# Order of two products of a pair in the feed forward, small compression products issued two at a time, and a shorter planning distance in the memory attention

## The chip, the cores and the metric

One Trainium2 chip, one core. The time is device microseconds (us) of one execution, the median over the runs shown. The work is spread by hand over TensorE (matrix products, PE in the profile; PEld is its weight load), VectorE (DVE), ScalarE (ACT), GpSimd (POOL) and SyncE (SP), which issues the transfers from memory.

## The reference, cut to what matters

Two models run one after the other on a 512 x 1024 activation: two layers of a first model, then a block of a second. The change touches three pieces of the second one.

```python
def _compress(tok, pos_emb, w1, w2):            # 512 tokens -> 31 blocks of 32 tokens
    idx = np.arange(n_cmp)[:, None] * CMP_STRIDE + np.arange(CMP_LEN)[None, :]
    blocks = tok[:, idx] + pos_emb
    hid = jax.nn.gelu(blocks.reshape(B, n_cmp, CMP_LEN * hd) @ w1)
    return hid @ w2

def _memory_attention(h, mem, g_q, g_kv, w_q, w_kv, w_o):   # 4 heads, 256 memory rows
    q = (_rmsnorm(h, g_q) @ w_q).reshape(B, S, MEM_HEADS, MEM_HEAD_DIM)
    kv = (_rmsnorm(mem, g_kv) @ w_kv).reshape(B, M, 2, MEM_HEADS, MEM_HEAD_DIM)
    pr = jax.nn.softmax(jnp.einsum('bshd,bmhd->bhsm', q, kv[:, :, 0]) * MEM_HEAD_DIM ** -0.5)
    o = jnp.einsum('bhsm,bmhd->bshd', pr, kv[:, :, 1])
    return o.reshape(B, S, MEM_HEADS * MEM_HEAD_DIM) @ w_o

def _swiglu(u, w_in, w_out):                    # D_FF = 2816, 22 blocks of 128
    a = u @ w_in
    return (jax.nn.silu(a[..., :D_FF]) * a[..., D_FF:]) @ w_out
```

## The kernel before, in words

Activations lie transposed, as eight tiles of 128 features x 512 tokens. A weight unit is a `raw` tile of 128 x 1024 that SyncE loads; ScalarE rounds it into `whi`, VectorE or GpSimd takes the rest into `wlo`, and each product of full precision is three products of TensorE: `xh,whi`, `xl,whi` and `xh,wlo`, accumulated in a bank of PSUM. Banks have three tags: three `mm`, four `x`, one `o`. Five stages follow each other: A and C (the first model), B (the mixer of the second), Q (memory attention), F (feed forward).

The whole program is planned while it is built. `Build` holds a model of the engines with a cost for every operation. The order on TensorE comes from the code: between two steps of a long projection `mms` calls `tick`, and there a generator waiting in `active` or `queue` (a step of some attention, say) may put its own products in. It may when `at(a) + self.margin <= self.now`: its inputs and a free bank must be there, by the model, at least `margin` ahead. `margin` is 2000 ns everywhere (`MARGIN`). Where no projection is left to hide behind, `drain` forces the steps. The other engines' orders come from a second pass (`again`), which works back from the end, gives every operation a latest time, and lets each engine take the most urgent one that is ready; additions and subtractions may land on VectorE or GpSimd. So any change of TensorE's order can move operations of the other engines far around it.

Three places matter.

`compress` (stage B, in `phase_b`), run for keys and for values: 16 products of 31 columns in single precision, `w1` (tiles `cw`) against the blocks `bl` (tile `blk`), into one bank with the tag x. In the trace each such product is two passes.

`phase_q` (stage Q): the two query projections `mq`, then `chain(j, i0)` four times (heads pair j, half i0 of the tokens): logits `ps_x<-memk,mq`, maximum, exponential, sum and scaling of `e` on VectorE and ScalarE, transposes `ps_x<-ident,e`, copies `pt`, products with the values `ps_o` or `ps_mm<-pt,memv`. Two projections of the memory (`mkv` 2 and 3, products `mxh,whi` of 256 columns) and the transposes of their result (`mvt`) come in the same stage.

`pair` (stage F): 17 pairs of units of the feed forward (`fa`, `fb`) are computed with seven products of 256 columns in place of eight. Each product n is 12 instructions of TensorE (4 x 3). `x[n]` holds its moving side (made once by `side`: `th`, `tl`, and for product 4 `zh`, `zl`), `it[n]` its weights (`wsh`, `wsl` for 6, 7 and 3, `whi`, `wlo` for the rest). Products 2 and 3 share a bank ("c"), 5 and 4 share another ("d"). After each product its result is added on VectorE: after 5, q's second half is `p + u` (in the trace `pp<-ps_x,pp`); after 3, t1 = bank c + q; after 4, t2 = bank d + u. Besides, two output products of the feed forward (`ps_mm<-acth,woh` and so on) stand between pairs.

Of the kernel before, what the change touches and what calls it, by code (L numbers as in the profile page):

```python
# [44 lines left out]
NEVER = 1e15  # L45
IDLE = {"V": 0.0, "A": 0.0, "G": 0.0, "D": 2150.0}
LOOK, NORMED_A = 2, 14
MARGIN = 2000.0
MEM_FROM, MEM_B = ("up", 1, 0), 2

QUEUED = {"V": 300, "A": 200}
# [278 lines left out]
class Build:  # L330
# [3 lines left out]
    def __init__(self, ctx, tc, aps, out):  # L334
# [7 lines left out]
        self.conc = 4  # L342
        self.margin = MARGIN
        self.o_free = PSUM_BUFS["o"]
# [564 lines left out]
    def pair(self, it, x, nxt):  # L909

        V, A = self.V, self.A
        a, b = slice(0, 256), slice(256, 512)
        if nxt:
            self.sums(nxt)
            self.whole(nxt, 0)
        while len(x[4]) < 4:
            assert self.force(), it["keys"]
        bank = lambda: self.p(min(("mm", "x"), key=lambda t: min(map(self.free, self.slots[t]))))
        t1, t2, q = self.t("pr"), self.t("pr"), self.t("pp")
        u = self.t("pp")  # L920
        banks = {}
        for n, name, c in ((1, "1", a), (2, "c", a), (6, "6", a), (5, "d", b), (7, "7", a), (4, "d", a), (3, "c", b)):
            if name not in banks:
                banks[name] = bank()
            p = banks[name]
            hi, lo = it.pop(n)
            for k in range(4):
                xh, xl = x[n][k]
                self.T.matmul(p[:, c], hi[:, k], xh, start=k == 0, stop=False)
                self.T.matmul(p[:, c], hi[:, k], xl, start=False, stop=False)  # L930
                self.T.matmul(p[:, c], lo[:, k], xh, start=False, stop=k == 3)
                self.tick()
            self.rank += EVAC
            if n == 1:
                A.copy(q[:, a], p[:, a])
            elif n == 6:
                V.tensor_add(u[:, a], p[:, a], q[:, a])
            elif n == 5:
                V.tensor_add(q[:, b], p[:, b], u[:, a])
            elif n == 7:  # L940
                V.tensor_add(u[:, b], p[:, a], u[:, a])
            elif n == 4:
                two = lambda t: t.rearrange("p (h c) -> p h c", h=2)
                V.tensor_add(two(t2), two(p), u[:, None, b].to_broadcast([P, 2, 256]))
            elif n == 3:
                V.tensor_add(t1, p, q)
            self.rank -= EVAC
            if n == 2:
                if nxt:
                    self.whole(nxt, 1)  # L950
                else:
                    self.ahead()
        return t1, t2
# [740 lines left out]
    def phase_b(self, h, prev):  # L1694
# [291 lines left out]
        def compress():  # L1986
            yield "need", ("r", "kvc")
            kvc = T["kvc"]
            w2, hidden, kv = self.t("cw2"), self.t("hid"), self.t("kvc")
            w2k, w2v = w2[:, :P], w2[:, P:P + 64]  # L1990
            self.dma(w2k, self.aps["cw2k"])
            self.dma(w2v, self.aps["cw2v"])
            hid, hu = (hidden[:, 64 * n:64 * n + 64].rearrange("p (b n) -> p b n", b=2) for n in range(2))
            hv4 = hidden[:, P:2 * P].rearrange("p (h n) -> p h n", h=4)
            kc.append(kv[:, :32])
            vc.append(kv[:, 32:288].rearrange("p (h n) -> p h n", h=4))
            G.memset(hid, 0.0)
            G.memset(vc[0], 0.0)
            for b in range(2):
                st, bl = self.t("cst"), self.t("blk")  # L2000
                r = slice(64 * b, 64 * b + 64)
                self.dma(st[:64], kvc[r])
                self.dma(st[64:, :S - 1], kvc[r, 1:])
                yield "on", st
                src = bass.AP(tensor=st.tensor, offset=st.offset, ap=[st.ap[0], [2, 16], [16, 31]])
                V.tensor_add(bl[:, :496].rearrange("p (l n) -> p l n", l=16), src,
                             col["pos_k" if b == 0 else "pos_v"][:, :, None].to_broadcast([P, 16, 31]))
                w1 = [self.t("cw1") for _ in range(4)]
                for c in range(4):
                    self.dma(w1[c].rearrange("p (l m) -> p l m", l=4),  # L2010
                                        self.aps["cw1k" if b == 0 else "cw1v"][:, 4 * c:4 * c + 4])
                yield "on", w1, bl
                p = self.p("x")
                for l in range(16):
                    mm(p[:, :31], w1[l // 4][:, (l % 4) * P:(l % 4 + 1) * P], bl[:, l * 31:(l + 1) * 31],
                       start=l == 0, stop=l == 15)
                V.tensor_copy(hid[:, b, :31], p[:, :31])
                yield
            V.tensor_mul(hu, hid, hid)
            V.tensor_scalar(hu, hu, 0.044715, 1.0, op0=OP.mult, op1=OP.add)  # L2020
            V.tensor_mul(hu, hu, hid)
            A.activation(hu, hu, AF.Tanh, scale=math.sqrt(2.0 / math.pi))
            V.scalar_tensor_tensor(hu, hu, 1.0, hid, op0=OP.add, op1=OP.mult)
            V.tensor_scalar_mul(hid, hu, 0.5)
            V.tensor_copy(hv4, hid[:, 1:2, :].to_broadcast([P, 4, 32]))
            yield "on", hid, hv4
            p = self.p("x")
            mm(p[:, :32], w2k, hid[:, 0], start=True, stop=True)
            V.tensor_copy(kc[0], p[:, :32])
            p = self.p("x")  # L2030
            mm(p[:, :64], hidden[:, P:2 * P], w2v, start=True, stop=True)
            for hh in range(4):
                V.tensor_copy(vc[0][32 * hh:32 * hh + 32, hh], p[32 * hh:32 * hh + 32, :64])
            yield "done", "kc"
            yield
# [105 lines left out]
        for w in MAIN_B.split():  # L2141
            k = int(w[-1]) if w[-1].isdigit() else 0
            n = w.rstrip("0123")
# [27 lines left out]
        for w in BACK_B.split():  # L2171
            k = int(w[-1]) if w[-1].isdigit() else 0
            n = w.rstrip("0123")
            if n == "st":
                for i in range(4):
                    self.add(stick(k, i), ("ka", k))
                self.add(tok(("va", k), ("van", k)), ("va", k))
            elif n == "tw":
                self.add(tok("vwgt", "vwg"), "vwgt")
            elif n == "tb":  # L2180
                self.add(tok("vbs", "vbn"), "vbs")
            elif n == "se":
                self.add(select(k), "vwg")
            elif n == "dsa":
                for i in range(4):
                    self.add(dsa(k, i), ("qb", k))
            elif n == "cp":
                self.add(compress(), "kvc")
                for i in range(4):
                    self.add(cmp_gen(i), "kvc")  # L2190
            elif n == "nsa":
                for i in range(4):
                    n = 4 * k + i - LOOK
                    self.add(nsa(k, i), "ksw" if n < 0 else ("npv", n // 4, n % 4))
# [15 lines left out]
    def phase_q(self, h, prev):  # L2210
        mm = self.T.matmul
        V, A = self.V, self.A
        x, rb = self.start(h, prev, self.col["norm_mq"], EPS6, "norm_q")
        self.conc = 4
        D, y = {}, {}
        halves = (slice(0, 64), slice(64, 128))

# [61 lines left out]
                self.add(chain(j, i0), ("mq", j))  # L2279
        self.tasks([(("mq", j), None, functools.partial(q_task, j)) for j in range(2)] + self.mem_tasks(range(MEM_B, 4)))  # L2280
        self.drain()
        hi, lo = self.unit(("mo", 0))
        begun = [self.p("mm") for _ in range(PSUM_BUFS["mm"] - 1)]
        for j, p in enumerate(begun):
# [17 lines left out]
    def phase_f(self, h, prev):  # L2302
# [58 lines left out]
        self.start_now(norm_x())  # L2361
        self.tasks([((key, f), None, functools.partial(into, f, key)) for f in range(PLAIN) for key in ("fa", "fb")][:-1])
        pairs = [pair(f) for f in range(PLAIN, FF)]
        self.sums(pairs[0])
        for _ in into(PLAIN - 1, "fb"):
# [117 lines left out]
```

## Time and profile before

| | |
|---|---|
| median of 3 runs | 1486.21 us (1485.58 to 1487.2) |
| the profiled execution | 1487.19 us, its span 1485.3 us |
| TensorE busy | 1460.9 us, 98% of the span, 8452 products |
| VectorE, ScalarE, GpSimd busy | 1075.7, 780.6, 366.4 us |
| granted TensorE clock, mean | 0.994 of full speed |
| chain that ended last | TensorE 87%, VectorE 7%, ScalarE 3% |

A row of a stage says how long the stretch is and how much of it each engine was busy; the length less PE's number is the time in which TensorE stood still. PEclk is the granted clock: 1.00 is 2.4 GHz, 0.50 is 1.2 GHz. In a timeline, brackets hold the idle time just before an instruction and the engine that ended it. Almost all instructions carry one line of a helper, so tiles tell them apart.

### The profile page before, as it was taken

The numbers are of one execution on the slowest core, as the hardware profiler recorded it, in microseconds if no ns is written. First come the engines' busy times: TensorE is split into PE (matmuls) and PEld (weight loads), VectorE is DVE, ScalarE is ACT, GpSimd is POOL, SyncE is SP. The second block draws the span as 40 slices with busy tenths as digits, with TensorE's granted clock in tenths as the row PEclk, the third lists the DMA queues.
The fourth block names the chain that finished last, engine by engine and source line by source line (L and its number), as shares of the span: only waits on it lengthen the run. The fifth ranks groups of instructions, "written<-read, shape, count | busy, mean of one in ns | idle before, by whom it ended". The sixth has DMA issues, their size and how long they took to land.

```text
span 1485.3 us, 22690 instructions
## 1 busy us (share of the span) xinstructions
PE 1460.9 (98%) x8452; PEld 1247.2 (84%) x8452; DVE 1075.7 (72%) x2081; ACT 780.6 (53%) x1548; POOL 366.4 (25%) x267
## 2 busy tenths in 40 slices
PE   8999999999999999999999999999999999999997
PEld 6888888888888888888887888888878899999986
DVE  6997877556535587666989994756566888877755
ACT  5553557555523588744688335754355544444324
POOL 1272612010100010000343030302015668532310
PEclk9999999999999999999999999999999999999998
DMA  6222222322332311124424331223312232332221
GB/s 218 85 72 71 80 92 71 100 85 86 114 114 100 103 64 65 58 96 139 123 89 129 119 118 61 86 72 132 124 57 88 83 128 93 107 128 100 75 82 58
DMA packets 53358, 143.52 MB, mean 97 GB/s; under 512 B 6848, under 2 KB 11968, under 8 KB 53248
## 3 DMA queue, kind: packets, MB, share of 16 engines
q1 hardware_dynamic: 53248, 142.07, 28.8%
q8 instruction: 67, 1.10, 0.3%
q14 instruction: 43, 0.35, 0.1%
HBM read 128.81 MB, written 4.19 MB: 90 GB/s over the span
## 4 chain that ended last, share of the span: by engine, by line
PE 87%; DVE 7%; ACT 3%; issue 1%; DMA 1%; POOL 0%; SPq 0%; POOLq 0%; DVEq 0%; ACTq 0%
PE ps_mm L595 64%; PE ps_x L595 19%; PE ps_o L595 4%; DVE sc L595 1%; ACT su L595 1%; DVE wlo L595 1%; DMA rpu<-rpr 1%; ACT e L595 1%; DVE sr L595 0%; ACT se L595 0%; ACT sr L595 0%; DVE e L595 0%; ACT whi L595 0%; DVE cv L595 0%; DVE m L595 0%
## 5 line engine op out<-in xcount | busy, mean ns | idle before, releaser
L595 PE MATMUL ps_mm<-xh,whi 128*128 128x512 f32 x936 | 383.7, 410 | 0.1
L595 PE MATMUL ps_mm<-xh,wlo 128*128 128x512 f32 x936 | 367.3, 392 | 0.0
L595 PE MATMUL ps_mm<-xl,whi 128*128 128x512 f32 x936 | 366.6, 392 | 0.0
L595 ACT CAST whi<-raw 128x1024 fp32r<-128x1024 f32 x199 | 208.7, 1052 | 256.3 <-issue 130.6
L595 DVE TENSOR_TENSOR wlo<-raw,whi 128x1024 fp32r<-128x1024 f32 x162 | 209.1, 1293 | 63.5 <-ACT whi L595 62.7
L595 PEld LDWEIGHTS ps_mm<-xh,wlo 128*128 128x128 f32 x936 | 176.2, 188 | 39.0
L595 PEld LDWEIGHTS ps_mm<-xh,whi 128*128 128x128 f32 x936 | 176.8, 189 | 32.9 <-issue 2.9
L595 PEld LDWEIGHTS ps_mm<-xl,whi 128*128 128x128 f32 x936 | 177.2, 189 | 28.4
L595 POOL TENSOR_TENSOR wlo<-raw,whi 128x1024 fp32r<-128x1024 f32 x37 | 91.9, 2484 | 152.7 <-ACT whi L595 152.5
L595 DVE TENSOR_TENSOR h<-ps_mm,h 128x512 f32<-128x512 f32 (+1 forms) x92 | 61.0, 665 | 84.1 <-PE ps_mm L595 84.0
L595 ACT ACTIVATE e<-e,nm 128x256 f32<-128x256 f32 (+3 forms) x176 | 92.7, 528 | 54.0 <-DVE nm L595 53.3
L595 POOL TENSOR_TENSOR rcol<-var,mhalf 128x4 f32<-128x4 f32 (+2 forms) x18 | 18.6, 1033 | 394.9 <-DVE var L595 375.5
L595 ACT COPY pt<-ps_x 128x384 f32<-128x384 f32 (+3 forms) x132 | 57.9, 457 | 47.9 <-PE ps_x L595 47.6
L595 PE MATMUL ps_mm<-acth,woh 128*128 128x512 f32 (+1 forms) x192 | 71.7, 373 | 0.0
L595 PE MATMUL ps_mm<-actl,woh 128*128 128x512 f32 (+1 forms) x192 | 71.5, 372 | 0.0
L595 PE MATMUL ps_mm<-acth,wol 128*128 128x512 f32 (+1 forms) x192 | 71.4, 372 | 0.0
L595 ACT CAST wsh<-ws 128x512 fp32r<-128x512 f32 x51 | 31.5, 619 | 56.1 <-DVE ws L595 48.4
L595 PE MATMUL ps_x<-ident,e 128*128 128x128 f32 x344 | 54.9, 282 | 1.7 <-DVE sm L595 0.7
L595 PE MATMUL ps_x<-th,wsh 128*128 128x256 f32 x192 | 54.3, 283 | 0.0
L595 PE MATMUL ps_x<-tl,wsh 128*128 128x256 f32 x192 | 54.3, 283 | 0.0
L595 PE MATMUL ps_x<-th,wsl 128*128 128x256 f32 x192 | 54.3, 283 | 0.0
L595 PEld LDWEIGHTS ps_x<-ident,e 128*128 128x128 f32 x344 | 43.0, 145 | 12.6 <-issue 1.6
(535 smaller groups left out, 3487.0 us busy)
## 6 DMA issues: line engine op xcount, KB each, us to landing
raw<-in_w_dram SPq DMA_DIRECT2D x199, 512.0 KB, 3.3
wo<-in_wo_dram SPq DMA_DIRECT2D x40, 256.0 KB, 3.7
h<-in_xt_dram SPq DMA_DIRECT2D x16, 256.0 KB, 3.7
kd<-pr SPq DMA_DIRECT2D x32, 128.0 KB, 2.3
rpu<-rpr SPq DMA_DIRECT2D x34, 64.0 KB, 2.0
park<-h SPq DMA_DIRECT2D x8, 256.0 KB, 3.0
h<-park SPq DMA_DIRECT2D x8, 256.0 KB, 5.3
out_dram<-h SPq DMA_DIRECT2D x16, 128.0 KB, 1.8
```

Source lines behind the costliest of these rows:

```text
L595: op.ways[op.lane][1]()
```

## The change

It does three things: in `pair`, product 3 is issued before product 4; in `compress`, the generator yields after every second product, so that the small products come two at a time wherever `tick` lets them in; and in `phase_q` the distance `margin` is 400 ns from the start of the stage until `drain` is over.

```diff
-MARGIN = 2000.0
+MARGIN, MARGIN_Q = 2000.0, 400.0
...
-        for n, name, c in ((1, "1", a), (2, "c", a), (6, "6", a), (5, "d", b), (7, "7", a), (4, "d", a), (3, "c", b)):
+        for n, name, c in ((1, "1", a), (2, "c", a), (6, "6", a), (5, "d", b), (7, "7", a), (3, "c", b), (4, "d", a)):
...
                 for l in range(16):
+                    if l and l % 2 == 0:
+                        yield
                     mm(p[:, :31], w1[l // 4][:, (l % 4) * P:(l % 4 + 1) * P], bl[:, l * 31:(l + 1) * 31],
...
         self.conc = 4
+        self.margin = MARGIN_Q
...
         self.drain()
+        self.margin = MARGIN
```

TensorE, stage B, the first of the two compressions (`blk,cw` are its products, `xh,whi` and the like belong to a projection). Before:

```order
L595 MATMUL ps_mm<-xh,wlo 128x512
L595 MATMUL ps_x<-blk,cw_1910 128x31 x4
L595 MATMUL ps_x<-blk,cw_1911 128x31 x4
L595 MATMUL ps_x<-blk,cw_1912 128x31 x4
L595 MATMUL ps_x<-blk,cw_1913 128x31 x4
L595 MATMUL ps_x<-ident,e 128x128 x2
L595 MATMUL ps_mm<-xh,whi 128x512
```

TensorE at the same place in the changed kernel:

```order
L595 MATMUL ps_mm<-xh,wlo 128x512
L595 MATMUL ps_x<-blk,cw_1910 128x31 x2
L595 MATMUL ps_mm<-xh,whi 128x512
L595 MATMUL ps_mm<-xl,whi 128x512
L595 MATMUL ps_mm<-xh,wlo 128x512
L595 MATMUL ps_x<-blk,cw_1910 128x31 x2
```

The run of 16 is cut into eight twos with at least three products of 512 columns between any two of them, in both compressions.

TensorE, stage Q, from the last of the memory projections to the first products with the values. Before:

```order
L595 MATMUL ps_x<-mxh,wlo 128x256
L595 MATMUL ps_x<-memk,mq 128x256 x4
L595 MATMUL ps_x<-mxh,whi 128x256
L595 MATMUL ps_x<-mxl,whi 128x256
L595 MATMUL ps_x<-mxh,wlo 128x256
L595 MATMUL ps_x<-ident,mvt 128x128 x2
L595 MATMUL ps_x<-memk,mq 128x256 x8
L595 MATMUL ps_x<-ident,mvt 128x128 x2
L595 MATMUL ps_x<-ident,e 128x128 x20
L595 MATMUL ps_x<-memk,mq 128x256 x4
L595 MATMUL ps_o<-pt,memv 64x128 x16
```

TensorE in the changed kernel, with the first logits further up (ahead of "..."):

```order
L595 MATMUL ps_mm<-mxh,wlo 128x256
L595 MATMUL ps_x<-memk,mq 128x256 x8
L595 MATMUL ps_mm<-mxh,whi 128x256
...
L595 MATMUL ps_x<-mxh,wlo 128x256
L595 MATMUL ps_x<-ident,e 128x128 x4
L595 MATMUL ps_x<-mxh,whi 128x256
...
L595 MATMUL ps_x<-ident,mvt 128x128 x2
...
L595 MATMUL ps_x<-ident,e 128x128 x8
L595 MATMUL ps_x<-memk,mq 128x256 x8
L595 MATMUL ps_o<-pt,memv 64x128 x16
```

The logits of the first two chains stand three steps into the first memory projection in place of seven steps into the second, the transposes of the first chain stand between steps of the second projection, and the logits of the last two chains come together.

TensorE, stage F, first pair: the end of product 7, then the first and last instructions of the two products that change places (`zh` is product 4, `th_2618` to `th_2642` with `wsh_2689` product 3; `ps_x_2729` is bank d, `ps_x_2725` bank c). Before:

```order
L595 MATMUL ps_mm_2730<-th_2640,wsl_2688 128x256
L595 MATMUL ps_x_2729<-zh_2612,whi_2699 128x256
...
L595 MATMUL ps_x_2729<-zh_2629,wlo_2700 128x256
L595 MATMUL ps_x_2725<-th_2618,wsh_2689 128x256
...
L595 MATMUL ps_x_2725<-th_2642,wsl_2690 128x256
```

In the changed kernel:

```order
L595 MATMUL ps_mm_2730<-th_2640,wsl_2688 128x256
L595 MATMUL ps_x_2725<-th_2618,wsh_2689 128x256
...
L595 MATMUL ps_x_2725<-th_2642,wsl_2690 128x256
L595 MATMUL ps_x_2729<-zh_2612,whi_2699 128x256
...
L595 MATMUL ps_x_2729<-zh_2629,wlo_2700 128x256
```

Twelve instructions now stand between the end of product 7 and the first instruction that writes bank d again.

VectorE at that place, before (`pp_2722<-ps_x_2729` reads bank d, that is product 5):

```order
L595 TENSOR_TENSOR pp_2723<-ps_x_2728,pp_2722 128x256
L595 TENSOR_TENSOR wlo_2718<-raw_2691,whi_2717 128x1024
L595 TENSOR_TENSOR pp_2722<-ps_x_2729,pp_2723 128x256
L595 TENSOR_TENSOR pp_2723<-ps_mm_2730,pp_2723 128x256
L595 TENSOR_TENSOR wsl_2713<-ws_2708,wsh_2712 128x512
```

And in the changed kernel:

```order
L595 TENSOR_TENSOR pp_2723<-ps_x_2728,pp_2722 128x256
L595 TENSOR_TENSOR ws_2708<-raw_2691,raw_2698 128x512
L595 TENSOR_TENSOR wlo_2718<-raw_2691,whi_2717 128x1024
L595 TENSOR_TENSOR pp_2722<-ps_x_2729,pp_2723 128x256
L595 TENSOR_TENSOR pp_2723<-ps_mm_2730,pp_2723 128x256
L595 TENSOR_TENSOR wsl_2713<-ws_2708,wsh_2712 128x512
```

A difference of weights (`ws`), which GpSimd took before, stands ahead of the read of bank d. Over stage F VectorE takes eight more such differences and three more `wlo` than before, and GpSimd as many fewer.

## Rows read from the trace of the kernel before

**Rows 1.** Stages of the whole span: length, busy time of each engine, PEclk, DMA.

```profile
core 0: us, PE busy (x) PEld busy (x) DVE busy (x) ACT busy (x) POOL busy (x), PEclk, DMA share, GB/s
0.00:50.00 50.00, 43.27 (x188) 34.45 (x189) 37.29 (x63) 28.11 (x46) 7.96 (x16) 1.00 0.53 183
50.00:800.00 750.00, 750.00 (x4129) 628.09 (x4128) 536.90 (x1099) 433.99 (x904) 143.94 (x106) 1.00 0.28 91
800.00:860.00 60.00, 58.06 (x329) 47.94 (x328) 57.36 (x170) 29.45 (x70) 14.32 (x10) 0.94 0.37 118
...
1075.00:1110.00 35.00, 31.71 (x234) 26.22 (x233) 19.34 (x43) 16.92 (x48) 3.36 (x2) 0.95 0.21 72
...
1175.00:1225.00 50.00, 46.60 (x343) 44.21 (x341) 44.99 (x58) 23.45 (x39) 32.60 (x18) 1.00 0.35 121
1225.00:1460.00 235.00, 235.00 (x1575) 217.84 (x1573) 176.20 (x239) 93.73 (x152) 92.30 (x60) 1.00 0.28 93
1460.00:1485.30 25.30, 16.62 (x135) 15.74 (x133) 11.72 (x31) 10.02 (x22) 2.38 (x3) 0.83 0.25 84
```

**Rows 2.** Short stretches of stage B, the same columns.

```profile
828.13:831.50 3.37, 2.91 (x8) 2.34 (x9) 3.37 (x16) 1.58 (x3) 0.00 (x0) 0.50 0.05 21
841.62:845.20 3.58, 3.58 (x34) 3.58 (x33) 3.58 (x12) 0.51 (x1) 0.00 (x0) 1.00 0.41 149
845.20:848.60 3.40, 3.40 (x11) 2.73 (x11) 2.96 (x12) 0.70 (x3) 0.61 (x2) 0.50 0.00 0
908.00:924.00 16.00, 16.00 (x130) 13.13 (x129) 5.60 (x12) 6.40 (x14) 0.00 (x0) 1.00 0.20 68
```

**Rows 3.** TensorE's timeline around the first compression: start, duration, instruction.

```profile
824.28 3.65 PE L595 MATMUL ps_x<-blk,cw 128*128 128x31 f32 x32
...
829.96 0.63 PE L595 MATMUL ps_mm<-xh,wlo 128*128 128x512 f32 x1
...
832.65 0.39 PE L595 MATMUL ps_mm<-xl,whi 128*128 128x512 f32 x1
832.88 0.39 PE L595 MATMUL ps_mm<-xh,wlo 128*128 128x512 f32 x1
```

**Rows 4.** Short stretches of stage Q, columns as in group 1.

```profile
1090.00:1097.80 7.80, 4.88 (x32) 3.30 (x33) 7.01 (x19) 7.15 (x28) 2.34 (x1) 1.00 0.22 69
1097.80:1101.20 3.40, 3.40 (x16) 2.99 (x17) 2.23 (x6) 2.17 (x6) 0.00 (x0) 0.50 0.33 129
```

**Rows 5.** Timelines of stage Q: TensorE, then ScalarE.

```profile
1091.72 2.30 PE L595 MATMUL ps_x<-memk,mq 64*128 64x256 f32 x16 [1.05 <-ACT e L595]
1095.61 0.44 PE L595 MATMUL ps_x<-ident,mvt 128*128 128x128 f32 x2 [1.59 <-DVE mx L595]
...
1102.68 0.47 ACT L595 ACTIVATE e<-ps_x,mx 128x256 f32<-128x256 f32 x1 [2.54 <-DVE mx L595]
```

**Rows 6.** TensorE's two waits in stage F.

```profile
1183.91 0.39 PE L595 MATMUL ps_x<-zh,whi 128*128 128x256 f32 x1 [1.91 <-DVE pp L595]
...
1211.40 0.39 PE L595 MATMUL ps_mm<-zh,whi 128*128 128x256 f32 x1 [1.49 <-DVE pp L595]
```

**Rows 7.** The chain of work that ended last, one product of a pair: start, us, what.

```profile
1213.10 1.44 PE ps_x L595 x12
```

**Rows 8.** VectorE's timeline in stage F.

```profile
1183.44 0.41 DVE L595 TENSOR_TENSOR pp<-ps_x,pp 128x256 f32<-128x256 f32 x1
...
1208.47 2.54 DVE L595 TENSOR_TENSOR ws<-raw 128x512 f32<-128x512 f32 x1
```

**Rows 9.** Stretches of one pair's length in stage F, columns as in group 1.

```profile
1196.54:1212.08 15.54, 14.05 (x95) 12.88 (x95) 14.79 (x16) 7.36 (x13) 12.51 (x8) 1.00 0.30 103
...
1243.16:1258.70 15.54, 15.54 (x110) 14.58 (x109) 13.89 (x15) 7.11 (x11) 14.67 (x10) 1.00 0.33 119
```

**Rows 10.** VectorE's groups from 1175 to 1430 us: busy and mean ns, idle before.

```profile
L595 DVE TENSOR_TENSOR wlo<-raw,whi 128x1024 fp32r<-128x1024 f32 x27 | 39.9, 1478 | 15.7 <-ACT whi L595 15.7
...
L595 DVE TENSOR_TENSOR ws<-raw 128x512 f32<-128x512 f32 x27 | 24.7, 913 | 0.3
```

## The prediction

> **What bounds the kernel now.** The first view is the table of stages [rows 1]. TensorE is the bound almost everywhere: from 50 to 800 us and from 1225 to 1460 us it is busy for the whole stretch. So a gain can come only from time in which TensorE stands still or runs at its lower clock, and the reader should look for stages where its number is under the length or PEclk is under 1.00. Five matter. The first 50 us (6.73 us idle) and the last 25 us (8.68 us) are the start and the tail, which the change does not reach. The three others hold its three edits: 800 to 860 us with 1.94 us idle and a clock of 0.94, 1075 to 1110 us with 3.29 us and 0.95, 1175 to 1225 us with 3.40 us at full clock [rows 1].
>
> The second view is the short stretches of those stages. In stage B, TensorE goes through 16 small products (32 passes) from 824.28 us in 3.65 us [rows 3] and through 16 more from 841.62 us. Right behind each run the clock falls to 0.50, that is from 2.4 to 1.2 GHz, for about 3.4 us: 828.13 to 831.50 and 845.20 to 848.60 [rows 2]. A product of 512 columns then lasts 0.63 us, and 0.39 us once the clock is back [rows 3]. In stage Q the clock falls from 1097.80 to 1101.20 us, and there the 7.8 us ahead had TensorE busy for only 4.88 us [rows 4].
>
> The third view is TensorE's timeline with its waits. In stage Q it waits 1.05 us for an exponential and 1.59 us for a maximum [rows 5]. In stage F it waits twice, 1.91 and 1.49 us, both times at the first instruction of product 4, for VectorE's read of the bank that product 5 left (`pp`) [rows 6]; these two are all 3.40 us of that stage.
>
> **The change part by part.** No instruction of TensorE is added or removed: 16 products become eight twos, the rest moves. What stays the same is not priced; the sum is what the three places lose today and would no longer lose.
>
> Small products (stage B). At 0.50 of the clock half of TensorE's busy time is lost: half of 2.91 us is 1.46 us, and half of 3.40 us is 1.70 us [rows 2], together 3.2 us. Cut into twos with three products of 512 columns between them, the mix is like that from 908 to 924 us, where stretches of small products with the values alternate with projections and the clock stays at 1.00 [rows 2]. So I take the whole 3.2 us; the bounds are nothing (the falls have another cause) and 3.2 us. The passes cost what they did: about 0.11 us each (3.65 us over 32) [rows 3]. The 1.94 us of idle time in this stage is left as it is: the planner's second pass orders VectorE anew there, the block sums `blk` go from VectorE to GpSimd, and the transfers of the second compression come behind other weight loads on SyncE's queue; the old waits may go and new ones may come, so this is plus or minus 1.9 us with no sign. Each compression now holds one of four banks for the time of its eight twos and the projections between them; what waits for that bank is a step of an attention, which `tick` lets in later, and not TensorE.
>
> Distance (stage Q). What can be won is the idle 3.29 us [rows 1] and half of the 3.40 us at half clock, 1.70 us [rows 4]: 5.0 us in all. The first chains' logits move to where projections still cover the softmax behind them. But the last two chains' logits now come together, after all projections: ScalarE then has eight exponentials of 0.47 us [rows 5], 3.8 us, and with the maximum ahead and the scaling behind about 5 us pass until the last `e` can be transposed, while TensorE has only the other logits, the products with the values of the first two chains and a few transposes, 3 to 4 us. Before, the last chain alone came late, with four exponentials. So I leave 1.5 to 2.5 us of waits in the stage, gain 1.4 us of the 3.29, and for the clock take half of 1.70 us, as the new sparse stretch at the end may bring the fall back. That is 2.3 us, with bounds of nothing and 5.0 us. Waits at the head of TensorE's queue could also grow, since a step now stands 1.6 us nearer to its inputs; behind such a step wait the memory projections, whose own evacuations are not urgent.
>
> Product 3 first (stage F). Product 3 writes the other half of bank c, which nobody has to read first. Its 12 instructions take 1.44 us [rows 7]. So the read after product 5 gets 1.44 us more: the waits of 1.91 and 1.49 us become 0.47 and 0.05 us, which is 2.9 us. Not all of it will stay. VectorE is busy 14.79 of 15.54 us in the second pair [rows 9], in the changed order a difference of weights stands ahead of the very read that TensorE waits for, and such an operation took 2.54 us in the third pair while it stood against GpSimd's work [rows 8]; the read of the first pair began at 1183.44 us, and a hold of that size would give back most of what the order wins. I take 2.0 us, with bounds of nothing and 3.4 us.
>
> The sum is 3.2 + 2.3 + 2.0 = 7.5 us. Against the profiled execution's 1487.19 us that gives 1479.7 us; this execution lies 0.98 us above the median of the runs, so the forecast is 1478.7 us, 0.5% faster. About 0.2% (3.0 us) is what a measurement of this kernel can tell from no change.
>
> **The rivals.** First, that the small products are not what lowers the clock. For it speaks that at the first fall TensorE had also just stood still, and in stage Q the fall follows an idle stretch [rows 4]. Against it speaks the second fall: from 841.62 to 845.20 us TensorE is busy without a gap, and the clock still falls [rows 2]. The time would be 1478.7 + 3.2 = 1481.9 us. The Trainium skill, page "TensorE: Matmul & The Clock Gate", section "Why this matters for your kernels", names idle gaps between bursts of products as what makes the throughput drop in mid-kernel. Taken by itself it would give this rival's time; the trace disagrees at 845.20 us, where no gap stands ahead.
>
> Second, that the waits of stages Q and F only move: the stage's other engines set its length, and what TensorE saves at one product it waits at the next. For it speaks VectorE's 14.79 of 15.54 us [rows 9] and the 7.01 and 7.15 us of 7.80 us for which VectorE and ScalarE are busy in stage Q [rows 4]. Against it speaks that from 1225 us on TensorE never waits [rows 1], so a lag of VectorE is caught up. Only the clock term is left: 1478.7 + 4.3 = 1483.0 us.
>
> Third, more is won than I take: all of 3.2, 5.0 and 3.4 us, 11.6 us, which gives 1474.6 us. For it speaks only that each of these losses has a named cause that the change moves.
>
> Fourth, nothing is won: new waits in stage B from the new order of VectorE, up to its 1.9 us, and those of the second rival, with a clock that falls elsewhere: 1486 us.
>
> Fifth, slower: VectorE becomes the bound of stage F. The order gives it three more `wlo` of 1.478 us and eight more `ws` of 0.913 us on average [rows 10], 11.7 us, and the other moves about cancel. If all of it lay on the path and the 2.0 us were lost too, the time would be 1478.7 + 2.0 + 11.7 = 1492.4 us. It decides where a pair asks VectorE for more than 15.54 us; spread over 16 pairs it is 0.7 us a pair, which takes 14.79 us to the limit but leaves 13.89 us [rows 9] below it. So it is unlikely.
>
> **How the numbers follow.** The chances: the forecast 0.50, the clock rival 0.12, waits that move 0.13, all won 0.10, nothing won 0.08, slower 0.07. The range from 1474.0 to 1485.0 us reaches from the case in which all is won to just short of the last two, which leaves some 0.19 outside with a little below. Faster by over 0.2% means under 1483.2 us: 0.50 + 0.12 + 0.10, and a good half of the waits that move, makes 0.80. Within 0.2%: the rest of those and the case of nothing won, 0.13. Slower: 0.07.
>
> **What would show it.** Right: in stage B no stretch with PEclk at 0.50 after the small products, which stand as eight rows of four passes, each about 0.44 us; in stage Q the first transposes of `e` between `mxh` products, and a wait left ahead of the last transposes; in stage F, `zh,whi` of the first and third pair with a wait under 0.7 us. Wrong: half clock again around 830 and 846 us (first rival), idle rows of `ps_x` in stage F of over 2 us that wait for `pr`, `wlo` or `wsl` (second and fifth), or idle time from 727 to 860 us that grew by over 2 us (fourth).

## The result, and the profile after

The changed kernel takes 1474.99 us, median of 5 runs (1474.38 to 1475.7); the kernel before, in the same comparison, 1485.58 us (1484.54 to 1487.2). The ratio is 0.9926 with a 95% interval of 0.9912 to 0.9939: 10.6 us faster, where 7.5 us were forecast; the time lies 1.0 us above the lower end of the range. The profiled execution took 1474.38 us, its span is 1472.6 us.

The stages of the changed kernel (columns and bounds as in [rows 1]):

```profile
core 0: us, PE busy (x) PEld busy (x) DVE busy (x) ACT busy (x) POOL busy (x), PEclk, DMA share, GB/s
0.00:50.00 50.00, 43.36 (x194) 34.39 (x195) 38.56 (x65) 29.04 (x47) 9.17 (x17) 1.00 0.52 183
...
800.00:860.00 60.00, 60.00 (x340) 50.09 (x338) 59.18 (x185) 29.11 (x68) 17.34 (x11) 1.00 0.42 134
...
1075.00:1110.00 35.00, 33.56 (x242) 28.08 (x242) 27.45 (x54) 25.81 (x64) 6.58 (x4) 1.00 0.23 74
...
1175.00:1225.00 50.00, 48.70 (x340) 45.43 (x339) 48.74 (x55) 22.67 (x38) 34.69 (x21) 1.00 0.32 116
```

In all three stages the idle time is down (1.94 to 0.00, 3.29 to 1.44, 3.40 to 1.30 us), and PEclk is 1.00 in the two where it was 0.94 and 0.95. TensorE's small products now stand between projections, and a product of 512 columns behind them takes 0.48 us at a granted clock of 1.00, where it took 0.63 us at 0.50 in [rows 3]:

```profile
820.91 0.53 PE L595 MATMUL ps_x<-blk,cw 128*128 128x31 f32 x4
821.27 0.48 PE L595 MATMUL ps_mm<-xh,whi 128*128 128x512 f32 x1
...
822.05 0.53 PE L595 MATMUL ps_x<-blk,cw 128*128 128x31 f32 x4
```

TensorE's waits of stage Q, against 1.05 and 1.59 us in [rows 5]:

```profile
1082.81 0.66 PE L595 MATMUL ps_x<-ident,e 128*128 128x128 f32 x4 [0.20 <-ACT e L595]
1091.65 0.41 PE L595 MATMUL ps_x<-ident,e 128*128 128x128 f32 x2 [0.19 <-DVE e L595]
1092.42 1.85 PE L595 MATMUL ps_x<-ident,e 128*128 128x128 f32 x10 [0.36 <-DVE e L595]
1095.45 0.44 PE L595 MATMUL ps_x<-ident,e 128*128 128x128 f32 x2 [0.44 <-ACT e L595]
```

TensorE's only long wait in the pairs of stage F. The two of [rows 6], in the first and the third pair, are gone, and a new one stands in the fourth pair (counted by the first `zh,whi` of each pair; the expectations below call it the third):

```profile
1216.31 0.39 PE L595 MATMUL ps_x<-zh,whi 128*128 128x256 f32 x1 [1.30 <-DVE pp L595]
```

VectorE just ahead of it:

```profile
1211.39 2.31 DVE L595 TENSOR_TENSOR wlo<-raw,whi 128x1024 fp32r<-128x1024 f32 x1
1213.62 1.77 DVE L595 TENSOR_TENSOR ws<-raw 128x512 f32<-128x512 f32 x1
1215.32 0.94 DVE L595 TENSOR_TENSOR pp<-ps_x,pp 128x256 f32<-128x256 f32 x2
```

To place the gain, the span is cut at instructions of TensorE that both kernels have: the transposes of `xs` near 47 us, the first `mgh,whi` behind stage B, the first `ymh,whi` behind stage Q, the first `th,whi` of stage F, the last transposes of `rcol`.

| profiled execution | xs to mgh (A, C, B) | mgh to ymh (Q) | th to rcol (F) | half clock in B, Q, F (us) |
|---|---|---|---|---|
| before | 979.99 | 80.34 | 302.42 | 6.8, 3.4, 0 |
| changed | 974.69 | 76.91 | 300.46 | 0, 0, 0 |
| difference | -5.30 | -3.43 | -1.96 | |

That is 10.7 us. The other 2.0 us between the two spans lie ahead of the first point (1.36 us) and behind the last (0.6 us), where nothing was changed.

### The profile page after: what moved, and what is told of

Same layout as the page of the kernel before. It is cut to its first block, busy times and chain, and to the rows that moved or that the text cites. A ratio compares the mean times of both kernels' runs of the same rounds, so it can differ in the third digit from the quotient of the medians.

```text
span 1472.6 us, 22699 instructions
## 1 busy us (share of the span) xinstructions
PE 1454.5 (99%) x8452; PEld 1242.6 (84%) x8452; DVE 1084.1 (74%) x2097; ACT 778.1 (53%) x1549; POOL 340.4 (23%) x250
## 4 chain that ended last, share of the span: by engine, by line
PE 96%; DVE 2%; ACT 1%; issue 0%; DMA 0%; POOL 0%; POOLq 0%; DVEq 0%; SPq 0%; ACTq 0%
PE ps_mm L595 70%; PE ps_x L595 21%; PE ps_o L595 5%; ACT e L595 1%; DVE cv L595 0%; DVE wlo L595 0%; DMA h<-in_xt_dram 0%; DVE B L595 0%; DVE sm L595 0%; DVE h L595 0%; DVE mx L595 0%; DVE ws L595 0%; DVE e L595 0%; POOL h L595 0%; ACT whi L595 0%
## 5 line engine op out<-in xcount | busy, mean ns | idle before, releaser
L595 DVE TENSOR_TENSOR wlo<-raw,whi 128x1024 fp32r<-128x1024 f32 x169 | 217.0, 1287 | 64.1 <-ACT whi L595 63.3
L595 POOL TENSOR_TENSOR wlo<-raw,whi 128x1024 fp32r<-128x1024 f32 x30 | 74.6, 2486 | 152.6 <-ACT whi L595 149.0
L595 ACT COPY pt<-ps_x 128x512 f32<-128x512 f32 (+3 forms) x132 | 57.1, 455 | 40.6 <-PE ps_x L595 40.4
L595 PE MATMUL ps_x<-th,wlo 128*128 128x256 f32 x168 | 47.5, 283 | 0.0
L595 PE MATMUL ps_x<-tl,whi 128*128 128x256 f32 x168 | 47.5, 283 | 0.0
L595 PE MATMUL ps_x<-th,whi 128*128 128x256 f32 x168 | 47.5, 282 | 0.0
```

The source lines that it names most:

```text
L595: op.ways[op.lane][1]()
```

## The experiments

Each of the 12 kernels is built from the kernel before or from the changed one. Times are medians, beside the kernel before in the same comparison: 1485.95 us for e1_order, e2_twos, e3_distance and e4_eights, 1485.5 us for n_order, n_distance, o_early5 and o_late7, 1486.1 us for e5_fours, n_twos, q0 and reads_first. The lengths of the table above, for all of them, and how long TensorE stood still and VectorE was busy from 727 to 860 us:

| kernel | xs to mgh | Q | F | half clock in B, Q, F | TensorE idle | VectorE busy |
|---|---|---|---|---|---|---|
| before | 979.99 | 80.34 | 302.42 | 6.8, 3.4, 0 | 1.94 | 125.09 |
| e1_order | 979.80 | 80.10 | 302.49 | 6.7, 3.4, 3.4 | 1.53 | 125.57 |
| e3_distance | 980.30 | 76.93 | 302.50 | 6.8, 0, 0 | 1.89 | 125.11 |
| n_twos | 979.76 | 76.93 | 300.81 | 0, 0, 0 | 3.72 | 125.68 |
| e4_eights | 980.27 | 80.17 | 303.08 | 3.4, 3.4, 0 | 2.95 | 125.43 |
| e5_fours | 980.26 | 79.78 | 304.03 | 0, 3.4, 3.4 | 4.03 | 125.50 |
| changed | 974.69 | 76.91 | 300.46 | 0, 0, 0 | 0.00 | 130.72 |
| e2_twos | 974.84 | 78.83 | 304.92 | 0, 0, 3.4 | 0.00 | 130.89 |
| n_order | 974.67 | 76.92 | 302.43 | 0, 0, 0 | 0.00 | 130.52 |
| n_distance | 975.43 | 80.34 | 302.80 | 0, 3.4, 3.4 | 0.29 | 130.56 |
| o_early5 | 974.99 | 76.92 | 302.86 | 0, 0, 3.4 | 0.08 | 130.46 |
| o_late7 | 975.22 | 76.93 | 305.71 | 0, 0, 3.4 | 0.15 | 130.47 |
| reads_first | 975.14 | 76.93 | 300.80 | 0, 0, 0 | 0.05 | 130.38 |
| q0 | 974.88 | 79.70 | 300.92 | 0, 3.4, 0 | 0.00 | 130.79 |

### One edit alone

**e1_order.** The order of products alone.

```diff
-(7, "7", a), (4, "d", a), (3, "c", b)
+(7, "7", a), (3, "c", b), (4, "d", a)
```

> Product 3 ahead of product 4 alone; the small products stand in runs of 16 and the distance is 2000 ns, as before. Steps add up (theory): the waits of 1.91 and 1.49 us on the read of bank d shrink, the wait of the third pair may stay; 1.9 to 2.1 us less than the kernel before (ratio 0.9986), and all stages ahead of the feed forward as before, with half clock at 828 and 845 us. Rival, VectorE only moves the wait: less than 0.7 us gained, and idle rows in the feed forward that add up to 2.7 us or more. Rival, planner's luck: the edit gains something by another order far from the feed forward, which stages ahead of 1175 us would show.

1484.64 us, ratio 0.9990 (0.9981 to 0.9999). The stages ahead of F are as before. In F the waits of the first and the third pair went, and 1.79 us came in the fourth. Behind that wait the clock fell:

```profile
1225.76 0.42 PE L595 MATMUL ps_x<-zh,whi 128*128 128x256 f32 x1 [1.79 <-DVE pp L595]
```

```profile
1226.00:1229.40 3.40, 3.40 (x15) 3.21 (x15) 2.78 (x5) 1.92 (x3) 2.54 (x2) 0.50 0.02 5
```

3.40 - 1.79 = 1.6 us less waiting, 1.7 us lost to the clock: F is as long as before in this execution. So the order did shorten the waits, and the fall took the gain back. From `th` to `rcol` the changed kernel, n_twos, n_distance and q0 have the same instructions in the same order on TensorE, VectorE, ScalarE and GpSimd as e1_order: the three without a fall there take 300.46 to 300.92 us, the two with one (e1_order and n_distance) 302.49 and 302.80 us. A fall costs 1.6 to 2.3 us here, about what the order wins.

**e2_twos.** The split of the small products alone.

```diff
+                    if l and l % 2 == 0:
+                        yield
```

> Small products two at a time alone. Theory (the run of 16 lowers the clock and also makes TensorE wait for the copy of transposed probabilities ahead of it): 800 to 860 us at a granted clock of 1.00, no half clock behind the small products, no wait of 1.28 us at 816 us; 4.5 to 5.5 us less than the kernel before (ratio about 0.9966). Rival, only the clock is from this edit and the waits of that stage went by the other edits' planning: 3.2 us less. Rival, idle gaps lower the clock and not the small products: half clock stays near 830 and 846 us and the gain is under 2 us.

1481.52 us, ratio 0.9962 (0.9950 to 0.9975). Up to `mgh` 5.15 us are won, and the changed kernel wins 5.30 us there, so this edit alone makes nearly the whole gain of stage B. In F it loses 2.5 us: product 4 still comes first there, and waits 2.17 and 2.36 us in the first and the third pair, the first of them with half clock behind it.

**e3_distance.** The 400 ns alone.

```diff
+        self.margin = MARGIN_Q
```

> The distance of 400 ns in the memory attention alone. Theory: the stage of the memory attention becomes 3.4 us shorter, no half clock at 1098 us, waits of TensorE there of 0.5 us or less each; 3.4 us less than the kernel before (ratio 0.9977). Rival, waits only move: the half clock goes and the idle time stays near 3 us, 1.7 us less. Rival, the three edits help each other (the planner orders the other engines anew over the whole program): alone under 1 us is gained.

1483.06 us, ratio 0.9980 (0.9971 to 0.9989). Q is 3.41 us shorter, without half clock; everything else is as before. The theory's 3.4 us stands.

**e4_eights** and **e5_fours.** As e2_twos, with a yield at every eighth and every fourth product.

```diff
+                    if l and l % 8 == 0:
+                        yield
```

> Small products eight at a time: two runs of 8 per compression, with at least three products of 512 columns between them, in place of eight runs of 2. Theory, length of the run lowers the clock: a run of 8 lasts 1.8 us, half of that before; if half clock comes back behind runs of 8, the loss is up to 3.2 us again and the gain is only the waits' 1.5 to 2 us; if not, 4.5 to 5.5 us are gained, as with twos. I expect no half clock (0.7), since between 908 and 924 us runs of small products of similar length leave it at 1.00. Rival, idle gaps lower the clock: half clock wherever TensorE stood still for more than 0.6 us just ahead, whatever the run's length.

> The kernel before with small products four at a time alone (four runs of 4 per compression). By the clock: no half clock behind the small products, as with twos and eights, 3.2 us. What TensorE's waits for e and pt between 815 and 835 us do is the planner's order: 2 us less idle as with twos or 2.4 us more as with eights; so 0 to 6 us less than the kernel before, and if there is a half clock it stands behind a wait of over 1.5 us and not behind small products.

Eights: 1488.84 us, ratio 1.0018 (1.0009 to 1.0027), slower, where 4.5 to 5.5 us less were expected without half clock. Fours: 1485.25 us, ratio 0.9995 (0.9986 to 1.0004), no change. Neither has half clock behind small products. The only fall of eights in B stands behind a wait of 1.85 us:

```profile
819.70 0.30 PE L595 MATMUL ps_x<-ident,e 128*128 128x128 f32 x1 [1.85 <-DVE e L595]
```

```profile
821.00:824.40 3.40, 3.40 (x11) 2.54 (x10) 2.27 (x8) 1.42 (x6) 0.00 (x0) 0.50 0.82 252
```

Fours have no half clock in B at all, and yet take 980.26 us up to `mgh`, as long as the kernel before. The clock was won, and the time was not: TensorE stands still 4.03 us in place of 1.94 us from 727 to 860 us, near the worse of the two cases that the expectation named. So the 3.2 us are not won by the clock alone; the planner's new order can take them back in waits.

### One edit left out

**n_order**, **n_distance**, **n_twos**: the changed kernel with the old order, with 2000 ns in stage Q, and without the yield. The edit of n_distance:

```diff
-MARGIN, MARGIN_Q = 2000.0, 400.0
+MARGIN, MARGIN_Q = 2000.0, 2000.0
```

> The changed kernel with product 4 ahead of product 3 again; twos and the distance of 400 ns stay. Theory A, the steps add up: the feed forward is as in the kernel before, 8.6 us less than the kernel before in all (ratio 0.9942). Theory B, the feed forward is planned anew after twos and a shorter lead into it, and without the order its waits at product 4 grow to some 4.5 us, as with the twos alone, with a chance of half clock behind one of them: 5 to 7 us less than the kernel before (ratio 0.9953 to 0.9966), so that the order is worth 4 to 5 us beside the other two and only 1.3 us by itself.

> The changed kernel with 2000 ns in the memory attention again; twos and the order stay. If the steps add up: 7.2 us less than the kernel before (ratio 0.9952), with the half clock and about 3 us of idle time in the memory attention back. If the distance also changes the feed forward by its other plan: off by over 1 us from that, to be seen at the first product 4 of each pair.

> The changed kernel with runs of 16 small products again; the order and the distance stay. If the steps add up, 5.3 us above the changed kernel and 5.3 us less than the kernel before: half clock for some 6.8 us around 830 and 846 us and waits of 1.28 and up to 0.66 us back, the memory attention 3.4 us shorter. Together with the two other kernels that leave one edit out it tells how far the three edits add up.

n_order: 1480.63 us (1477.83 to 1481.92), ratio 0.9965 (0.9951 to 0.9978). Its profile is that of its fastest run: F has the waits of [rows 6] again, 1.90 and 1.51 us, without half clock, 2.0 us more than the changed kernel. Every engine's order in F is that of the kernel before, so theory B (F planned anew) falls; but by the median only 4.9 us are won, not theory A's 8.6. Why its other runs are up to 4 us longer, no trace shows. n_distance: 1478.8 us, ratio 0.9955 (0.9943 to 0.9968), 6.7 us where 7.2 were expected; Q is as long as before, half clock included. n_twos: 1481.29 us, ratio 0.9968 (0.9956 to 0.9979), 4.8 us where 5.3 were expected.

n_twos also bears on what the clock costs in stage B. Up to stage Q, every engine has the same instructions in the same order in it as in the kernel before, in e1_order and in e3_distance; these are four executions of one program. In the three others the clock fell for 6.7 to 6.8 us in all. In n_twos it did not fall, although its small products stand in runs of 16:

```profile
824.70:840.00 15.30, 14.40 (x84) 12.09 (x83) 15.30 (x53) 7.11 (x21) 1.98 (x2) 1.00 0.32 102
840.00:850.00 10.00, 9.23 (x61) 8.26 (x62) 9.62 (x35) 3.48 (x10) 1.18 (x3) 1.00 0.16 53
```

Its length up to `mgh` is 979.76 us, against 979.80 to 980.30 us with the falls. This looks as if the clock were worth nothing, but the comparison is not clean. Counted from `xs`, n_twos is 0.78 us behind the kernel before at the same instruction near 773 us, by a wait for `sr` some 50 us ahead of any fall. It then gains 1.2 us where the first fall is missing, loses 1.16 us at TensorE's wait for VectorE's `e` ahead of the second run, a wait that the kernel before does not have there, gains 1.47 us where the second fall is missing, and gives back 0.5 us by 873 us.

```profile
840.77 0.70 PE L595 MATMUL ps_x<-ident,e 128*128 128x128 f32 x4 [0.98 <-DVE e L595]
```

Behind that wait stands VectorE's scaling of `e` beside a difference of weights on GpSimd. In the kernel before, GpSimd's `wlo` starts when the scaling is nearly done, and the two instructions take 0.60 us; in n_twos `wlo` starts 0.46 us ahead of them, and they take 2.33 us. Before, then n_twos:

```profile
838.15 0.60 DVE L595 TENSOR_SCALAR e<-e,sm 128x256 f32<-128x256 f32 x2
838.74 2.40 POOL L595 TENSOR_TENSOR wlo<-raw,whi 128x1024 fp32r<-128x1024 f32 x1 [1.03 <-ACT whi L595]
...
838.64 2.33 DVE L595 TENSOR_SCALAR e<-e,sm 128x256 f32<-128x256 f32 x2
838.18 2.38 POOL L595 TENSOR_TENSOR wlo<-raw,whi 128x1024 fp32r<-128x1024 f32 x1
```

So the equal lengths do not show that the clock is free in this order of the engines: n_twos got back some 2.7 us where the falls are missing, and lost some 2.4 us to a late start and to waits. Whether a faster TensorE brings such waits about, or they fell together by chance, one execution can't tell. The runs without a trace point to a small price. Of the 11 runs of e3_distance, five have a mean granted clock of 0.998 and a median of 1482.87 us, three 0.997 and 1482.69 us, three 0.996 and 1483.55 us; 0.002 of the clock is some 3.0 us of the span, by an estimate from these numbers, and where the clock fell in these runs is not recorded.

What the twos win shows in the rows from `xs` to `mgh` (columns as in [rows 1]): the kernel before, n_twos, fours, the changed kernel.

```profile
47.47:1027.46 979.99, 977.66 (x5497) 817.52 (x5498) 709.39 (x1557) 556.00 (x1167) 193.46 (x143) 1.00 0.28 92
47.17:1026.93 979.76, 975.64 (x5497) 815.15 (x5498) 710.06 (x1557) 555.76 (x1167) 193.69 (x143) 1.00 0.29 92
46.36:1026.62 980.26, 975.98 (x5498) 814.87 (x5498) 711.54 (x1551) 554.39 (x1166) 203.53 (x150) 1.00 0.29 92
46.11:1020.80 974.69, 974.30 (x5498) 815.20 (x5499) 708.55 (x1564) 554.33 (x1167) 186.06 (x136) 1.00 0.28 93
```

In the changed kernel TensorE is busy 974.30 of 974.69 us: it sets the length. Against the kernel before, its busy time is down by 3.36 us, about half of the 6.8 us at half clock, and its idle time by 1.94 us (2.33 to 0.39); together that is the 5.30 us. n_twos and fours have no half clock either, but their idle time grew to 4.12 and 4.28 us, and TensorE's busy time is 1.3 and 1.7 us above the changed kernel's; what these last are, the rows don't say. So the clock's term is kept only where the waits go too, and that is a matter of the other engines' order.

VectorE is the nearest of these. Its busy time from 727 to 860 us is 125.1 to 125.7 us where the stage is long and 130.4 to 130.9 us where it is short. By itself this says little: a faster execution has more of the program inside these fixed bounds, and from `xs` to `mgh` VectorE's busy time is nearly the same (709.39 and 708.55 us). Besides, the 14 executions are only four programs up to `mgh`: runs of 16 (four executions), eights, fours, and twos (eight executions). VectorE's waits there, in the kernel before (engine, tile, what it waited for: us in all, times, the longest):

```profile
DVE sc L595 <- ACT su L595: 2.6, 4, 0.7
DVE rp L595 <- POOL rpu L595: 2.1, 1, 2.1
DVE gm L595 <- PE ps_mm L595: 1.2, 1, 1.2
DVE sm L595 <- ACT e L595: 1.1, 2, 0.7
DVE ec L595 <- PE ps_x L595: 0.2, 1, 0.2
```

In n_twos:

```profile
DVE rp L595 <- POOL rpu L595: 2.9, 1, 2.9
DVE sc L595 <- ACT su L595: 2.6, 4, 0.7
DVE sm L595 <- ACT e L595: 1.1, 2, 0.7
```

And in the changed kernel:

```profile
DVE sc L595 <- ACT su L595: 0.7, 1, 0.7
DVE sm L595 <- ACT e L595: 0.6, 1, 0.6
DVE gm L595 <- PE ps_mm L595: 0.2, 1, 0.2
```

Of about 7 us of waits only 1.4 us are for TensorE, and none in n_twos: VectorE is held by GpSimd and ScalarE more than by TensorE. With twos the waits shrink to 1.5 us; up to `mgh` VectorE has seven instructions more than before and GpSimd seven fewer, while with fours VectorE has six fewer and GpSimd seven more. That VectorE's order is what takes TensorE's waits away is argued from these rows; no run changed it alone in stage B.

### The distance once more

**q0.** The changed kernel with 0 in place of 400 ns.

> The changed kernel with a distance of nothing in place of 400 ns in the memory attention. If the shorter distance wins by letting steps in while projections still stand behind them: as the changed kernel within 0.5 us or up to 0.7 us better. If steps now reach the head of TensorE's queue ahead of their inputs (the cost model is never exact): more waits of 0.3 to 1 us at the transposes of e, 1 to 2 us above the changed kernel.

1478.13 us, ratio 0.9947 (0.9935 to 0.9960), about 3 us above the changed kernel, where 1 to 2 us were expected if steps come too early. Q takes 79.70 us. The steps now come too early, TensorE waits at the head of its queue, and the clock falls behind it:

```profile
1094.56 0.83 PE L595 MATMUL ps_x<-ident,e 128*128 128x128 f32 x4 [1.19 <-ACT e L595]
```

So the distance can be too long and too short, and 400 ns is better than 0 and 2000 ns.

### The last wait of stage F

**o_early5** and **o_late7**: the changed kernel with other orders of the seven products. The edit of o_early5:

```diff
-(1, "1", a), (2, "c", a), (6, "6", a), (5, "d", b), (7, "7", a), (3, "c", b), (4, "d", a)
+(1, "1", a), (6, "6", a), (5, "d", b), (2, "c", a), (7, "7", a), (3, "c", b), (4, "d", a)
```

> The changed kernel with product 2 moved behind product 5 as well (1, 6, 5, 2, 7, 3, 4), so that the read of bank d has 4.3 us in place of 2.9 us until product 4 writes it. Theory, the wait of 1.30 us in the third pair is a read that comes too late behind other work of VectorE: it becomes nothing, and the time is 1.3 us under the changed kernel, 11.9 us less than the kernel before. Rival, VectorE is full in the first three pairs and its backlog decides: the wait comes back at another read of the same stretch, and the time is that of the changed kernel within 0.7 us or above it.

> The changed kernel with product 3 ahead of product 7 (1, 2, 6, 5, 3, 7, 4). The read of bank d has the same 2.9 us until product 4 writes it, so by the distance of the bank alone it is the changed kernel within 0.7 us, with a wait of about 1.3 us in the third pair. What differs from that is what another plan of VectorE's work by itself makes of the feed forward: I expect up to 2 us either way.

o_early5: 1477.21 us, ratio 0.9942 (0.9929 to 0.9954). o_late7: 1479.81 us, ratio 0.9962 (0.9949 to 0.9974). o_late7 is slower than the changed kernel, and o_early5 by its median too, though its interval overlaps with that of the changed kernel; the read of bank d has no less time in either. The wait on the read is gone in o_early5, and a longer one has come in the second pair, for weights that VectorE hasn't made yet, again with half clock behind it:

```profile
1179.56 0.39 PE L595 MATMUL ps_mm<-th,wsl 128*128 128x256 f32 x1 [2.73 <-DVE wsl L595]
```

**reads_first**: the changed kernel with one instruction of VectorE moved, the `wlo` at 1211.39 us behind the reads `pp`. VectorE's order there:

```diff
 TENSOR_TENSOR wsl<-ws,wsh 128x512
-TENSOR_TENSOR wlo<-raw,whi 128x1024
 TENSOR_TENSOR ws<-raw 128x512
 TENSOR_TENSOR pp<-ps_x,pp 128x256 x2
+TENSOR_TENSOR wlo<-raw,whi 128x1024
```

> The changed kernel with one instruction of VectorE moved: in the third pair of the feed forward the difference of weights wlo, 2.31 us, that stood ahead of the two reads pp (products 6 and 5) comes behind them; every other order on every engine stays. Theory, TensorE's last wait of 1.30 us there is this read standing behind that difference: the wait goes and nothing waits for the later wlo; 1.3 us under the changed kernel, 11.9 us less than the kernel before. Rival, VectorE has more to do than fits there: TensorE waits 1 us or more for the moved wlo or for the next read, and the time is that of the changed kernel.

1475.89 us, ratio 0.9931 (0.9918 to 0.9943): the changed kernel's time. The theory of 1.3 us falls. The wait is halved, and a second one comes three pairs later, at a read of the same kind:

```profile
1216.79 0.39 PE L608 MATMUL ps_x<-zh,whi 128*128 128x256 f32 x1 [0.63 <-DVE pp L608]
...
1264.42 0.38 PE L608 MATMUL ps_mm<-zh,whi 128*128 128x256 f32 x1 [0.44 <-DVE pp L608]
```

Together with the two orders this speaks for VectorE's backlog, and not one late read, as what bounds the first pairs: each time the wait moved to another instruction that VectorE owed.

## Why the prediction was right, and where it was not

**The sum.** Forecast 7.5 us, measured 10.6 us by the medians and 10.7 us by the stretches; the time lies in the range. In the changed kernel all three losses went as argued; the terms of B and Q were too small, and the gains hang in part on falls of the clock that come in one execution and not in another. The signs of being right came true: no half clock behind the small products, the first transposes of `e` between `mxh` products, waits under 0.7 us at product 4 of the first and the third pair.

**Small products (3.2 us for the clock, idle time plus or minus 1.9 us).** Measured 5.30 us, the top of these bounds: 3.36 us by the clock and 1.94 us of idle time. The term that was mis-sized is the idle time, "plus or minus 1.9 us with no sign"; it went whole. And "So I take the whole 3.2 us" came out right but was not safe: fours are rid of the half clock, eights of half of it, and neither gains, since TensorE's waits grow. The sum has the two terms as independent, and they are not: with eights and fours one grew as the other shrank. The prediction named the planner's new order of VectorE in this stage; VectorE's 57.36 of 60 us in [rows 1] said how little room it had. That the order came out well is luck as far as the prediction goes: nothing in it tells twos from fours. Why the planner finds the better order with twos and not with fours or eights is not settled; no run separates the order on TensorE from that on VectorE.

**The first rival** (small products do not lower the clock, 1481.9 us) is not what happened either. Behind runs of 16 the clock fell in three of four executions, at four of their eight runs. In e1_order it fell while the run was still going on: the run goes from 823.79 to 828.08 us, and the half clock begins at 826.6 us.

```profile
826.60:833.30 6.70, 6.66 (x22) 5.41 (x22) 6.70 (x24) 2.86 (x7) 0.00 (x0) 0.50 0.13 36
```

Behind runs of eight, four and two it never fell. Half clock also stands behind waits: of 15 waits of 1.6 us or more in the feed forward of all kernels, 6 (of 1.79 to 2.73 us) had half clock behind them and 9 (of 1.63 to 2.36 us) had not. That idle gaps lower the clock is what the Trainium skill says, page "TensorE: Matmul & The Clock Gate", section "Why this matters for your kernels"; these six go that way, at gaps shorter than those that the section warns of, and the runs of 16 stand beside them.

**Distance (2.3 us).** The mechanism held, the size was low: 3.43 us. Of the two parts, the clock was taken at half, 0.85 us, and idle time at 1.4 us. In this stage six executions have the same order on TensorE, VectorE, ScalarE and GpSimd (before, e1_order, e2_twos, e4_eights, e5_fours, n_distance). Five of them have the half clock and take 79.78 to 80.34 us; e2_twos, by chance, has none and takes 78.83 us, with waits of 1.05 and 1.59 us as before. So the clock is worth 1.0 to 1.5 us here. The idle time fell by 1.85 us (3.29 to 1.44 us). The fear that "the new sparse stretch at the end may bring the fall back" came true at 0 ns, not at 400 ns.

**Product 3 first (2.0 us).** Measured 1.96 us in the changed kernel, by the reckoning of the prediction: both waits at product 4, of the first and the third pair, went, and 1.30 us came back in the fourth. That this gain stayed is in part luck: by the same order in e1_order and n_distance the clock fell behind the wait that was left, and F is as long as before. The stretch that the prediction calls the second pair [rows 9] holds the wait at 1211.40 us, so it is the third. The second rival, waits that only move, is right in its mechanism for this stage and wrong in its price: a part moves. That VectorE's operation would be held where it stands against GpSimd is in the rows: `wlo` takes 2.31 us at 1211.39 us, beside 4.06 us of GpSimd's `actl`, and 1.48 us on average in [rows 10]; the prediction had a `ws` there.

**The fifth rival** (VectorE becomes the bound of F) did not come, but o_late7 shows that it was near: another order of the same products makes F 5.25 us longer than in the changed kernel, 1.7 us of it by half clock (half of 3.4 us).

**All won (1474.6 us).** The time is close to this rival's, its working is not: it had 3.2 us in B, 5.0 in Q and 3.4 in F; the stretches give 5.3, 3.4 and 2.0.

**Do the edits add up?** Alone they win 1.3, 4.4 and 2.9 us, 8.6 us of 10.6. The stretches show where the rest is: in B and Q each edit wins the same alone and together (5.15 and 5.30, 3.41 and 3.43 us), in F the order alone won nothing in its profile and 1.96 us with the others, by a fall of the clock that one execution has and another has not. Left out of the changed kernel, the edits cost more than they win alone: by the ratios some 5.8 us for the order, 4.3 us for the distance and 6.2 us for the twos, each give or take 2 to 3 us.

## What to carry to other kernels

Price a lower clock together with the waits beside it: here a regained clock was kept where the waits went too, and was lost to longer waits with fours. An edit of one engine's order in a planned program is an edit of all the others' orders: read what changed on the engine that has little room. A wait that is left can cost more than its length, so a gain counts as safe only when the waits that remain are short. And before two executions of one program are set against each other, line them up instruction by instruction: equal ends can hide a gain and a loss.

## What the runs showed of the hardware

The half clock comes in stretches of 3.4 us (e4_eights at 821.0, q0 near 1096, e1_order at 1226.0 us) or of 6.7 to 6.8 us (e1_order and e3_distance in B, where one such stretch stands in place of the two of 3.4 us in [rows 2]). Whether the same instructions draw it differs from one execution to the next: runs of 16 drew none in n_twos, a wait of 1.79 us had one behind it and one of 2.36 us none, and in stage Q the waits of 1.05 and 1.59 us had one in five executions and none in e2_twos. VectorE's scaling of a tile of 128 x 256 took 0.34 us where GpSimd's `wlo` began behind it, and 2.07 us in n_twos, where `wlo` had begun 0.46 us ahead.
